# Wider pieces for the first two tiles of an input projection, norm weights by DMA, low parts on VectorE, and other PSUM places where the search begins

## The chip, the cores and the metric

The kernel runs on one core of a Trainium2 chip. Its engines are TensorE (PE; its weight loads are listed as PEld), VectorE (DVE), ScalarE (ACT), GpSimd (POOL) and SyncE (SP, which issues most transfers). The metric is the device time of one execution in microseconds; the time of a kernel is the median of its runs.

## The reference

One layer of a streaming-encoder block on 4096 tokens of width 1024, in float32:

```python
h = rms_norm(x, norm_g[layer])
proj = h @ w_in[layer]
q, k, v, qi, ki, wi, z_a, u_b, z_b, gates = jnp.split(proj, SPLIT_POINTS, axis=-1)
q = apply_partial_rope(rms_norm(q, q_norm_g[layer]), cos_a, sin_a)
k = apply_partial_rope(rms_norm(k, k_norm_g[layer]), cos_a, sin_a)
qi = apply_partial_rope(qi, cos_i, sin_i) * (IDX_DIM ** -0.5)
ki = apply_partial_rope(ki, cos_i, sin_i)
a = dsa_attention(q, k, v, qi, ki, wi, k_sel) * jax.nn.silu(z_a)     # top 256 keys of each query
b = multiscale_pool(u_b, pool_w, pool_scale) * jax.nn.silu(z_b)
y = g[:, :, 0] * (a @ w_branch_a) + g[:, :, 1] * (b @ w_branch_b)    # g: sigmoid of the gates
x = x + y @ w_out
```

The change lies in the first two lines, and there in the columns of q (512), k and v (256) and of the indexer (qi, ki and wi, 296).

## The kernel before, in words

The program has four phases: phase 1 (norm, and the projections to q, kv and the indexer's columns), the search (phase_index: index scores, the threshold of the top 256, and beside it the projections to gates and pools), attention, and output. Phase 1 goes over 32 tiles of 128 tokens.

Each float32 product is made from parts: a high part, rounded to the type that TensorE reads (F32R), and the low part that is left. A tile's h is in `hh` (high) and `hl` (low), weights are in `wqh`, `wql`, `wkvh`, `wkvl`, `wih`, `wil`; a product is hh·wh + hl·wh + hh·wl. With 1024 rows, eight k-steps of 128, each of the three is a pass of eight matmuls.

A tile t goes like this. `load_x` fetches x. `stats` squares it on ScalarE (`sq`, L451), takes the root (`rsqrt`, L383 to L390) and scales x on VectorE by that and by the norm weights `gn` (L460). `transp` turns it in two halves on TensorE (L473, into PSUM tiles `pt`), copies each half to `hh` on ScalarE (L475) and the rest to `hl` on VectorE (L476); SP stores both to `hD`. Then come the matmuls into the PSUM tiles `ma` (q and kv, 768 of 1024 columns) and `mb` (indexer), and `evac` reads these out: squares for the head norms (L548), the root (on POOL), the scaling L557, which is the last reader of `ma`, the rotation on POOL (L573 to L576) with the tables `trig`, and stores. `ma`, `mb` and `pt` have two places each, so tile t + 2 needs what tile t has left.

Tiles 2 to 31 multiply whole parts (`project`, `mm3`: 512, 256 and 296 columns in a matmul, L401 to L403). For tiles 0 and 1 the weights are still arriving: `weights` loads them in pieces of 128 columns (L502; the last one has 40), splits each into high (ScalarE, L503) and low (L506; for q's pieces 0 and 2 on POOL, for the others on VectorE), and `piece` multiplies piece by piece (L524).

`begin` does what comes ahead: constants, 18 matmuls of zeros (L301), and the norm weights, which are loaded as one row (L306, ScalarE's queue), spread over the partitions by two TensorE matmuls with a row of ones (L311, into a tile of `ma`) and copied to `gn` (L313). `tables` makes the cos and sin tables `trig` by a chain of VectorE instructions (L341 to L373) and a sine on ScalarE (L376).

The order of the instructions on each engine is set by `Plan`: each step has an engine, a cost in estimated microseconds and a key; a list scheduler goes through time, and whenever an engine is free it takes the step with the lowest key whose inputs and tiles are there. Engines then run their rows strictly in that order. PSUM places of phase 1 are given out as tiles are first made: before, `pt0` has bank 0, `ma0` banks 1 and 2, `pt1` bank 3, `ma1` 4 and 5, `mb0` and `mb1` 6 and 7. The search lays its own PSUM tiles over these in the order of the loop over `pl.have` in `phase_index`; a step on such a tile waits for the last reader of what lay there. `pd` holds the gate projections (L1196 to L1198), `ps` the scores.

## Time and profile before

| | us |
|---|---|
| runs (3) | 4132.86, 4133.96, 4137.76; median 4133.96 |
| profiled execution, its time | 4135.42 |
| its span, first to last instruction | 4133.7 |
| mean granted TensorE clock | 0.985 |
| tile 2 of phase 1 begins on TensorE | 73.91 |
| phase 1's last matmul | 452.47 |
| the search's first gate matmul | 456.48 |

Instruction rows give start, length, engine, line, operation, tiles out<-in, shapes and, in brackets, the idle time ahead and what ended it. A row's length on TensorE overlaps the next row's; the rate is read from the starts. Tables by stage give the busy time of each engine in a window, with the granted TensorE clock as a share of full speed.

### The profile page before, as it was taken

What the parts mean: (1) busy time and instruction counts of PE and PEld (TensorE: products, weight loads), DVE (VectorE), ACT (ScalarE), POOL (GpSimd) and SP (SyncE); (2) the same over time, 40 slices, a digit from 0 to 9 for tenths busy, and PEclk for the clock granted to TensorE, in tenths of its full rate; (3) what the DMA queues carried; (4) which work ended last, traced back from release to release, by engine and by line L of the source; (5) the groups of instructions that cost most, each with busy time, mean ns of one, the idle gap of its engine ahead of it and who ended that gap; (6) DMA issues with size and microseconds to landing.
All of it is one profiled execution on the core that took longest, in us unless ns stands there. A gap on an engine that the chain in (4) does not pass through costs nothing.

```text
span 4133.7 us, 64472 instructions
## 1 busy us (share of the span) xinstructions
PE 4012.3 (97%) x23202; PEld 3074.1 (74%) x23203; DVE 3251.7 (79%) x6399; ACT 2259.5 (55%) x3163; POOL 2022.9 (49%) x1618
## 2 busy tenths in 40 slices
PE   9999999999999999999989999999999999999999
PEld 9999888787777777788756666666666666887787
DVE  5555688888888888778779999999999996556654
ACT  4444578786777877877645555555554543111221
POOL 3555312212213223010018889999999994334653
PEclk9999999999999999999979999999999999999999
DMA  6876644544545345666554433333222215887543
GB/s 183 301 244 237 201 168 173 171 167 168 177 164 194 135 172 180 199 234 237 199 142 87 76 76 61 64 62 54 56 54 43 40 25 167 284 254 239 190 158 122
DMA packets 515846, 636.87 MB, mean 154 GB/s; under 512 B 230593, under 2 KB 365377, under 8 KB 511554
## 3 DMA queue, kind: packets, MB, share of 16 engines
q1 hardware_dynamic: 490432, 609.51, 47.1%
q10 hardware_dynamic: 25090, 23.21, 2.5%
q8 instruction: 183, 3.00, 0.3%
q14 instruction: 141, 1.16, 0.1%
HBM read 408.96 MB, written 191.76 MB: 145 GB/s over the span
## 4 chain that ended last, share of the span: by engine, by line
PE 37%; DVE 6%; issue 4%; DMA 1%; POOL 1%; SPq 1%; ACT 0%; ACTq 0%; DVEq 0%; POOLq 0%
PE pv L1686 9%; PE st L1634 8%; PE p L2139 7%; PE p L1990 7%; PE ps L1566 4%; DVE jk L1575 4%; DVE tt L1647 1%; PE pt L1734 1%; PE pt L395 1%; DMA qm<-maxD 1%; PE st L395 0%; PE st L1854 0%; POOL g L2020 0%; DVE w L1897 0%; DMA g<-w_out 0%
## 5 line engine op out<-in xcount | busy, mean ns | idle before, releaser
L1665 POOL TENSOR_TENSOR acc<-acc,tt 128x1024 f32<-128x1024 f32 x388 | 927.7, 2391 | 64.0 <-ACT tt L1646 36.9
L1646 ACT ACTIVATE tt<-tt 128x1024 f32<-128x1024 f32 (+1 forms) x544 | 561.1, 1034 | 549.7 <-DVE tt L1647 518.9
L1197 PE MATMUL pd<-h,wgh 128*128 128x512 f32 x1792 | 708.8, 396 | 9.9 <-DMA h<-hD 9.9
L1196 PE MATMUL pd<-h,wgh 128*128 128x512 f32 x1792 | 714.1, 399 | 3.9 <-issue 3.8
L908 DVE SCALAR_TENSOR_TENSOR ring<-rl,wi,ring 128x1024 f32<-128x1024 f32 (+7 forms) x624 | 702.1, 1170 | 15.7 <-ACT rl L906 12.4
L1198 PE MATMUL pd<-h,wgl 128*128 128x512 f32 x1792 | 707.0, 395 | 0.0
L906 ACT ACTIVATE rl<-ps 128x1024 f32<-128x1024 f32 (+7 forms) x624 | 535.5, 887 | 190.0 <-PE ps L903 69.4
L1647 DVE TENSOR_TENSOR tt<-st,bT 128x1024 f32<-128x1024 f32 (+1 forms) x504 | 600.8, 1193 | 13.1 <-PE st L1634 13.1
L993 ACT ACTIVATE sg<-ring,tk 128x2048 fp8e4<-128x2048 f32 (+9 forms) x322 | 485.1, 1508 | 63.0 <-DVE tk L981 34.4
L1686 PE MATMUL pv<-tt,vv 128*64 128x256 f32 x4224 | 516.2, 386 | 1.4 <-ACT ov L1707 1.4
L1575 DVE CUSTOM_DVE_ANT_1 jk<-ps,bias,mf 128x1024 bf16<-128x1024 f32 (+3 forms) x408 | 469.6, 1151 | 17.1 <-PE ps L1566 15.3
L1686 PEld LDWEIGHTS pv<-tt,vv 128*64 128x64 f32 x4224 | 286.5, 137 | 168.7 <-issue 35.4
L1197 PEld LDWEIGHTS pd<-h,wgh 128*128 128x128 f32 x1792 | 339.8, 190 | 84.1 <-DMA h<-hD 16.6
L1196 PEld LDWEIGHTS pd<-h,wgh 128*128 128x128 f32 x1792 | 340.0, 190 | 78.6 <-issue 4.2
L1198 PEld LDWEIGHTS pd<-h,wgl 128*128 128x128 f32 x1792 | 339.4, 189 | 75.9
L903 PE MATMUL ps<-kis,qT 128*128 128x512 f32 (+3 forms) x1136 | 345.3, 390 | 37.9 <-ACT rl L906 37.7
L1990 PE MATMUL p<-g,w 128*128 128x512 f32 x1488 | 345.5, 394 | 1.7 <-DVE g L1913 1.7
L1990 PEld LDWEIGHTS p<-g,w 128*128 128x128 f32 x1488 | 279.4, 188 | 67.6 <-DVE g L1913 2.1
L2139 PE MATMUL p<-w,g 128*128 128x512 f32 x1344 | 314.3, 396 | 4.0 <-ACT g L2143 3.1
L2139 PEld LDWEIGHTS p<-w,g 128*128 128x128 f32 x1344 | 253.5, 189 | 64.6 <-ACT g L2143 3.5
L1566 PE MATMUL ps<-kh,qh 64*128 64x512 f32 (+3 forms) x1320 | 265.5, 419 | 29.3 <-DVE mf L1575 26.5
L1110 POOL COPY halo<-u 128x16 f32<-128x16 f32 x32 | 11.2, 350 | 575.5 <-ACT u L1104 575.5
(364 smaller groups left out, 7012.3 us busy)
## 6 DMA issues: line engine op xcount, KB each, us to landing
h<-hD SPq DMA_DIRECT2D x384, 512.0 KB
g<-gD SPq DMA_DIRECT2D x80, 512.0 KB
hlD<-rhl SPq DMA_DIRECT2D x31, 1216.0 KB
gD<-sgm SPq DMA_DIRECT2D x128, 256.0 KB
q<-hlD SPq DMA_DIRECT2D x61, 512.0 KB
x<-x SPq DMA_DIRECT2D x32, 512.0 KB
hD<-hh SPq DMA_DIRECT2D x32, 512.0 KB
hD<-hl SPq DMA_DIRECT2D x32, 512.0 KB
```

Of the source, the lines that this page charges most:

```text
L906: r = pl.add("act", 0.05 + n * 0.834e-3, k_, lambda ps=ps, rl=rl, n=n: act.activation(rl.t[:, :n], ps.t[:, :n], AF.Relu), [m], use=[ps, rl])
L908: prev[o] = pl.add("dve", 0.1 + n * 1.04e-3, k_, lambda rl=rl, o=o, n=n, h=h: v.scalar_tensor_tensor(acc[:, o:o + n], rl.t[:, :n], self.wi ...
L1196: pe.matmul(out, wh.t[:, k], r1, start=(k == 0), stop=False)
L1197: pe.matmul(out, wh.t[:, k], r2, start=False, stop=False)
L1198: pe.matmul(out, wl.t[:, k], r1, start=False, stop=(k == KT - 1))
L1575: v.tensor_tensor_reduce(out=jk.t[:, :2 * (hi - lo) * P].rearrange("p (t n) -> p t n", t=2), in0=flat().rearrange("p (t n) -> p t n", t=2) ...
L1646: act.activation(tt.t[:, 0:n], tt.t[:, 0:n], AF.Exp)
L1647: ad = last_ve[0] = pl.add("dve", 0.07 + 0.54 * n, key, lambda: v.tensor_tensor(tt.t[:, 0:n], s.t[:, 0:n], bc(bt.t[:, 2 * p:2 * p + n, Non ...
L1665: gp.tensor_tensor(acc.t, first, tt.t, op=OP.add)
L1686: pe.matmul(pv.t[64 * f:64 * f + 64], vv[:, k, 64 * g:64 * g + 64], T[u, p].t[:, k % 2, 2 * f:2 * f + 2], start=(k == 0), stop=(k == b))
L1990: pe.matmul(p.t, blk[i].t[:, k, ms], two(x[k // 2][j].t, F32R)[:, k % 2], start=(k == i == j == 0), stop=(k == 3 and i == 1))
L2139: pe.matmul(p.t, quarter(Q.t, x, F32R)[:, k], blk[y].t[:, k], start=(fresh and k == x == y == 0), stop=(k == 3 and x == 1), skip_group_che ...
```

## The change

Pieces are still loaded and split by 128 columns, but for tiles 0 and 1 `piece` now takes a list of them: q in two halves of 256, kv whole (256), the indexer's columns whole (296). A pass over high weights waits for the highs of its pieces, the low pass for their lows. All lows are on VectorE. The norm weights come by one DMA on SP's queue that reads the row 128 times into `gn`; the row of ones, the two matmuls and the copy are gone. The loads of x1 to x3 stand at other places among the weights. The search's PSUM tiles are laid out in another order.

```diff
-ON_POOL = {("q", 0), ("q", 2)}
...
-        row = xp.tile([1, P], F32, name="onerow")
-        s = pl.add("dve", 0.2, -100, lambda: (v.memset(one, 1.0), v.memset(row, 1.0)))
+        s = pl.add("dve", 0.1, -100, lambda: v.memset(one, 1.0))
...
-        x, ma = new("x"), new("ma")
-        g = pl.add("dma", 0.1, -101, lambda: act.dma_start(x.t[0:1], a["norm_g"]), use=[x])
-
-        def spread():
-            for f in range(2):
-                fs = slice(f * 512, f * 512 + 512)
-                pe.matmul(ma.t[:, fs], row, x.t[0:1, fs], start=True, stop=True)
-        g = pl.add("pe", 1.8, -60, spread, [g, s], use=[x, ma])
-        return pl.add("dve", 1.2, -60, lambda: v.tensor_copy(gn, ma.t), [g], use=[ma])
+        return pl.add("dma", 1.7, -95, lambda: dma(gn, bass.AP(tensor=a["norm_g"].tensor, offset=a["norm_g"].offset,
+                                                              ap=[[0, P], [1, D]])))
...
-                on = "pool" if (key, j) in ON_POOL else "dve"
-                eng = {"dve": v, "pool": po}[on]
-                l = pl.add(on, (2.4 if on == "pool" else 1.15) * n + 0.1, at, lambda: eng.tensor_tensor(
+                l = pl.add("dve", 1.15 * n + 0.1, at, lambda: v.tensor_tensor(
                     lo[:, :, o:e], raw, hi[:, :, o:e].bitcast(F32), op=OP.subtract), [h])
...
-            def piece(t, key, j, at, prev):
+            def piece(t, key, js, at, prev):
                 m, c = out_of(t, key)
-                o, e, hi, lo = pieces[key][j]
+                parts = [pieces[key][j] for j in js]
+                o, e = parts[0][0], parts[-1][1]
+                hi, lo = [x[2] for x in parts], [x[3] for x in parts]
...
-                for i, (x, w, after) in enumerate(((hh, wh, high + [hi]), (hl, wh, low), (hh, wl, [lo]))):
+                for i, (x, w, after) in enumerate(((hh, wh, high + hi), (hl, wh, low), (hh, wl, lo))):
...
-                    prev = pl.add("pe", 8 * 0.5e-3 * max(e - o, 64), at, mm, after + [prev], use=[m, hh, hl])
+                    prev = pl.add("pe", 8 * 0.4575e-3 * (e - o), at, mm, after + [prev], use=[m, hh, hl])
...
-            first = (("q", 0), ("q", 1), ("x", 1), ("q", 2), ("q", 3), ("x", 2), ("kv", 0), ("kv", 1), ("x", 3), ("i", 0), ("i", 1),
-                     ("i", 2))
+            first = (("q", 0), ("q", 1), ("q", 2), ("x", 1), ("q", 3), ("kv", 0), ("kv", 1), ("x", 2), ("i", 0), ("i", 1),
+                     ("i", 2), ("x", 3))
...
-            for n, (key, j) in enumerate(x for x in first if x[0] != "x"):
+            for n, (key, js) in enumerate((("q", (0, 1)), ("q", (2, 3)), ("kv", (0, 1)), ("i", (0, 1, 2)))):
                 for t in range(2):
-                    last[t] = piece(t, key, j, n + t * 2.5, last[t])
-                    if (key, j) == ("kv", 1):
+                    last[t] = piece(t, key, js, 2 * n + t * 2.5, last[t])
+                    if key == "kv":
                         ends[t] = last[t]
-                if key == "kv":
-                    transp(2, j, n + 2.0)
-                elif key == "i" and j < 2:
-                    transp(3, j, n + 4.0)
+                        transp(2, t, 2 * n + t + 2.0)
+                    elif key == "i":
+                        transp(3, t, 2 * n + t + 4.0)
...
-        for name, i in (("ps", 0), ("pd", 0), ("pd", 1), ("pd", 2), ("pt", 0), ("ps", 1)):
+        for name, i in (("pt", 0), ("pd", 0), ("pd", 1), ("pd", 2), ("ps", 0), ("ps", 1)):
```

What the scheduler makes of it shows in the order of the rows. From tile 2's first matmul on, TensorE's rows are the same as before one for one; on the other engines the rows differ for a few tiles more and are then the same to the end. TensorE from the matmuls of zeros on, first before and then now (names carry the number of the place; `hh1` and `hl0` are tile 0's):

```order
L301 MATMUL pt0_146<-hh0_138 128x512 x4
L311 MATMUL ma0_154<-x0_140,onerow_103 128x512 x2
L301 MATMUL pt0_146<-hh0_138 128x512 x14
L473 MATMUL pt1_193<-ident_68,x1_142 128x128 x4
L473 MATMUL pt0_202<-ident_68,x1_142 128x128 x4
L524 MATMUL ma1_213<-wqh_104,hh1_194 128x128 x8
L524 MATMUL ma1_213<-wqh_104,hl0_195 128x128 x8
L524 MATMUL ma1_213<-wql_105,hh1_194 128x128 x8
```

```order
L299 MATMUL pt0_142<-hh0_136 128x512 x18
L464 MATMUL pt1_181<-ident_68,x0_138 128x128 x4
L464 MATMUL pt0_189<-ident_68,x0_138 128x128 x4
L515 MATMUL ma0_203<-wqh_103,hh1_182 128x256 x8
L515 MATMUL ma0_203<-wqh_103,hl0_183 128x256 x8
L515 MATMUL ma0_203<-wql_104,hh1_182 128x256 x8
```

The two matmuls on the row of ones are gone from among the zeros, the passes are twice as wide, and tile 0 is in `ma0` instead of `ma1`, so that tile 31 is in `ma1` instead of `ma0`. With no matmul into `ma0` ahead of the first transposes, `pt1` also gets bank 1, `ma0` banks 2 and 3.

TensorE where phase 1 ends and the search begins, before and now, with the engines and queues that a row waits for:

```order
L403 MATMUL mb1_5465<-wih_108,hl1_5144 128x296
L395 MATMUL mb1_5465<-identr_69,rhk2_5292 128x128 [waits DVE_49]
L1196 MATMUL pd0_5599<-h0_128,wgh0_5277 128x512 [waits DMAHW7_49,DVE_49,Activation_49]
L1197 MATMUL pd0_5599<-h1_129,wgh0_5277 128x512 [waits DMAHW1_49]
L1198 MATMUL pd0_5599<-h0_128,wgl0_5278 128x512
L395 MATMUL pt0_5603<-identr_69,k30_73 128x128
```

```order
L394 MATMUL mb1_5218<-wih_107,hl1_4897 128x296
L386 MATMUL mb1_5218<-identr_69,rhk2_5045 128x128 [waits DVE_49]
L1186 MATMUL pd0_5352<-h0_127,wgh0_5030 128x512 [waits DMAHW1_49]
L1187 MATMUL pd0_5352<-h1_128,wgh0_5030 128x512 [waits DMAHW2_49]
L1188 MATMUL pd0_5352<-h0_127,wgl0_5031 128x512
L386 MATMUL pt0_5356<-identr_69,k30_73 128x128 [waits DVE_49,PE_49]
```

The rows are the same; `pd0` lay on bank 2, the kv half of tile 31's `ma0`, and lies on bank 1, which was `pt1`. Its first matmul no longer waits for VectorE and ScalarE. `pd1` and `pd2` lie on banks 2 and 3 (now tile 30's `ma0`), the first `ps` on tile 31's `ma1`.

VectorE in the middle of the table chain (`ang`, `nh`, `nl`), before and now, with the low part of tile 3's h (`hl0`):

```order
L357 SCALAR_TENSOR_TENSOR ang_122<-nh_124,ang_122 128x384
L357 SCALAR_TENSOR_TENSOR ang_122<-nl_125,ang_122 128x384
L476 TENSOR_TENSOR hl0_792<-pt1_790,hh1_791 128x512
L360 SCALAR_TENSOR_TENSOR ang_122<-n_123,ang_122 128x384
L476 TENSOR_TENSOR hl0_792<-pt0_824,hh1_791 128x512
L363 COPY r2_126<-ang_122 128x32x12
```

```order
L323 TENSOR_SCALAR gqk_79<-gq_119 128x512
L324 COPY gqk_79<-gq_119 128x128
L348 SCALAR_TENSOR_TENSOR ang_121<-nh_123,ang_121 128x384
L348 SCALAR_TENSOR_TENSOR ang_121<-nl_124,ang_121 128x384
L467 TENSOR_TENSOR hl0_562<-pt1_560,hh1_561 128x512
L467 TENSOR_TENSOR hl0_562<-pt0_568,hh1_561 128x512
```

Tile 3's lows stood after six of the `ang` steps and now stand after two, so that four of them, and all that follows in the chain, come behind tile 3's transposes.

## The prediction

> **What bounds the kernel now.** I read the page's busy shares, then the stages, then TensorE's rows in order of time, since an engine with 97% over 4.1 ms says nothing on the first 75 us, where the change lies.

> ```profile
> PE 4012.3 (97%) x23202; PEld 3074.1 (74%) x23203; DVE 3251.7 (79%) x6399; ACT 2259.5 (55%) x3163; POOL 2022.9 (49%) x1618
> ```

> By stages (window in us, its length, busy time of each engine with instruction counts, granted TensorE clock, DMA share, GB/s):

> ```profile
> 5.00:20.00 15.00, 14.50 (x76) 10.82 (x74) 11.20 (x19) 8.06 (x14) 4.77 (x2) 1.00 1.13 320
> 14.00:53.50 39.50, 39.44 (x353) 39.26 (x352) 24.76 (x44) 15.77 (x29) 6.62 (x17) 1.00 0.63 183
> 53.50:55.40 1.90, 1.90 (x20) 1.90 (x18) 1.76 (x5) 0.87 (x2) 0.00 (x0) 0.99 0.61 209
> 55.40:75.80 20.40, 20.40 (x94) 20.01 (x94) 3.14 (x7) 3.07 (x6) 1.89 (x3) 0.50 0.05 5
> 75.80:440.00 364.20, 364.20 (x2332) 332.77 (x2331) 205.32 (x413) 173.52 (x431) 203.39 (x521) 1.00 0.75 259
> 452.70:456.40 3.70, 0.00 (x0) 0.00 (x0) 2.20 (x6) 1.75 (x9) 1.63 (x11) 0.77 0.48 195
> 456.50:461.50 5.00, 5.00 (x12) 3.86 (x13) 3.61 (x7) 1.98 (x6) 4.84 (x10) 0.50 0.16 57
> 500.00:720.00 220.00, 220.00 (x975) 179.41 (x974) 182.73 (x448) 175.32 (x199) 36.85 (x33) 1.00 0.46 166
> ```

> TensorE has work without a break from 14 us to 452.7, and again from 500 to 720. So what is saved ahead of tile 2 is kept, unless another engine falls behind. But from 55.4 to 75.8 the granted clock is 0.50, and a busy TensorE there is half a TensorE. What a matmul costs is read from start to start (the rows' own lengths overlap):

> ```profile
> 33.99 1.05 PE L524 MATMUL ma<-wqh,hh 128*128 128x128 f32 x8
> 41.14 1.06 PE L524 MATMUL ma<-wql,hh 128*128 128x128 f32 x8
> 42.03 0.62 PE L473 MATMUL pt<-ident,x 128*128 128x128 f32 x4
> 42.41 1.09 PE L524 MATMUL mb<-wih,hh 128*128 128x128 f32 x8
> 53.58 1.01 PE L524 MATMUL mb<-wih,hh 128*128 128x40 f32 x8
> 54.44 0.82 PE L524 MATMUL mb<-wih,hl 128*128 128x40 f32 x6
> 73.91 0.78 PE L401 MATMUL ma<-wqh,hh 128*128 128x512 f32 x1
> 87.45 0.39 PE L401 MATMUL ma<-wqh,hh 128*128 128x512 f32 x1
> 100.07 0.46 PE L401 MATMUL ma<-wqh,hh 128*128 128x512 f32 x1
> 440.76 0.44 PE L401 MATMUL ma<-wqh,hh 128*128 128x512 f32 x1
> 446.30 0.28 PE L401 MATMUL ma<-wkvh,hh 128*128 128x256 f32 x1
> 449.17 0.30 PE L401 MATMUL mb<-wih,hh 128*128 128x296 f32 x1
> 452.47 0.22 PE L395 MATMUL mb<-identr,rhk 128*128 128x128 f32 x1
> ```

> Eight passes of eight 128-column matmuls lie between 33.99 and 41.14: 0.894 us a pass, 112 ns a matmul. A pass of 40 columns costs as much (53.58 to 54.44: 0.86). Tile 31 has 24 matmuls of each width: 512 columns 231 ns (440.76 to 446.30), 256 columns 120 ns (to 449.17), 296 columns 137 ns (to 452.47). So a piece of 256 costs 8 ns more than one of 128. Four transposes cost 0.38 (42.03 to 42.41). Tiles 2, 3 and 4 begin at 73.91, 87.45 and 100.07: 12.62 a tile, and 0.9 more in tile 2, which begins at the low clock.

> [...]

> **The change, part by part.** *Wide pieces.* Before, two tiles took 48 passes of 128 columns and 6 of 40; now 18 of 256 (0.957) and 6 of 296 (1.10), 23.8 us. When can they run? The rows that time the start:

> ```profile
> 4.56 1.06 ACT L451 ACTIVATE sq<-x 128x1024 bf16<-128x1024 f32 x1 [1.51 <-DMA x<-x]
> 7.16 1.23 DVE L313 COPY gn<-ma 128x1024 f32<-128x1024 f32 x1 [5.34 <-PE ma L311]
> 9.68 3.62 DVE L460 SCALAR_TENSOR_TENSOR x<-x,rs,gn 128x512 f32<-128x512 f32 x2
> 9.71 2.39 POOL L506 TENSOR_TENSOR wql<-h,wqh 128x1024 fp32r<-128x1024 f32 x1 [8.15 <-ACT wqh L503]
> 15.65 1.05 ACT L503 ACTIVATE wqh<-h 128x1024 fp32r<-128x1024 f32 x1
> 19.79 0.75 DVE L460 SCALAR_TENSOR_TENSOR x<-x,rs,gn 128x512 f32<-128x512 f32 x1
> 20.46 1.22 DVE L506 TENSOR_TENSOR wql<-h,wqh 128x1024 fp32r<-128x1024 f32 x1
> 21.32 0.60 ACT L475 ACTIVATE hh<-pt 128x512 fp32r<-128x512 f32 x1 [2.55 <-PE pt L473]
> 22.32 0.68 DVE L476 TENSOR_TENSOR hl<-pt,hh 128x512 fp32r<-128x512 f32 x1
> ```

> x0 lands at 4.56; at 320 GB/s each 512 KB behind it takes 1.64 us. In SP's new order that puts the norm weights at 6.2, q0 to q2 at 7.8, 9.5 and 11.1, x1 at 12.8, q3 at 14.4, kv at 16.0 and 17.7, x2 at 19.3, the index columns by 23.1, x3 at 24.8. ScalarE in its new order (1.05 a split, 0.60 a turned half): first splits done 8.9, turned tile 0 at 10.6, q1 11.7, q2 12.7, square of x1, q3 at 15.9, kv 17.1 and 18.8, turned tile 1 by 19.4. VectorE: from the copy's end at 8.39 to the scaling at 9.68 the root chain takes 1.3; without that copy x0 is scaled by 8.5; the lows of q1 and q2 are done by 14.4, x1 is scaled by 18.4. TensorE: three passes 11.7 to 14.6, a wait for q3 to 15.9, q's other three and tile 1's transposes (the last at 18.8) to 19.75. From there nothing it needs is late: 12 passes of 256, 6 of 296, 4 times 0.38 make 19.6, so tile 2 begins at 39.4 instead of 73.91, at full clock, and tile 3 at 52.0 instead of 87.45: **35.4 us earlier**. Bounds: 36 if only q3's split held it (15.9 plus 23.2 of work left); 31.5 if every landing is 1.64 late and a half-clock stretch like that of 456.5 to 461.5 costs 2.2 (6.1 less 3.9, below).

> *Norm weights by DMA.* 512 KB ahead of the weights instead of 4 KB, two TensorE matmuls and a copy. Nearest row: an x tile, 1.64 us, already in the landings (between 0, if 128 reads of one row are cheap, and 3.3). *Lows on VectorE.* Two of 2.39 on POOL become two of 1.22 on VectorE (counted above); POOL no longer slows VectorE, whose two scalings took 3.62 beside POOL's first low instead of 2 x 0.75. *SP* moves x1 to x3 behind weights and the first hD stores; their landings are counted.

> *What is late next.* The cos/sin tables (VectorE) and tile 2's read-out, which frees the PSUM tile that tile 4 needs:

> ```profile
> 49.70 0.17 DVE L341 CAST pos<-pos_i 128x32 f32<-128x32 int32 x1
> 55.98 0.56 DVE L357 SCALAR_TENSOR_TENSOR ang<-nl,ang 128x384 f32<-128x384 f32 x1
> 75.53 0.35 DVE L363 COPY r<-ang 128x384 f32<-128x384 f32 x1
> 81.61 0.55 DVE L373 TENSOR_SCALAR r<-r 128x768 f32<-128x768 f32 x1
> 83.24 0.85 ACT L376 ACTIVATE trig<-r 128x768 f32<-128x768 f32 x1
> 93.69 0.81 DVE L557 TENSOR_TENSOR row<-ma,ss 128x640 f32<-128x640 f32 x1
> ```

> Now the table is there at 84.1 and tile 2's PSUM free at 94.5, 10.4 later, with tile 4 at 100.07: 5.6 of slack. After: the tables begin behind hl of tile 2's second half (transposed at 34.9, so 36.7), take 6.8 (49.70 to 56.54), 0.6 and 6.6 (75.53 to 82.16), less the 1.0 of sums of squares that now stands earlier, plus two hl of 0.68: 51.1; ScalarE's table load and sine end at 53.1; PSUM is free at 63.5, and tile 4 wants it at 39.4 + 25.2 = 64.6. That leaves 1.1, and POOL beside VectorE can take it: **1 us lost** (0 to 4). Behind TensorE's wait there, all of phase 1 is queued.

> *PSUM at the search's begin.*

> ```profile
> 455.55 0.82 DVE L557 TENSOR_TENSOR row<-ma,ss 128x640 f32<-128x640 f32 x1 [1.18 <-POOL ss L390]
> 456.48 0.76 PE L1196 MATMUL pd<-h,wgh 128*128 128x512 f32 x1 [3.78 <-issue]
> 461.77 0.40 PE L1196 MATMUL pd<-h,wgh 128*128 128x512 f32 x1
> ```

> pd0 lay on tile 31's ma0, so its first matmul began 0.1 after L557 had read it (456.37), and the idle 3.8 cost the clock as well. Now pd0 lies on pt1, free long before. From 452.6, 12 matmuls at 231 ns and a transpose bring TensorE at 455.7 to where it was at 461.77: **6.1 us** (3.9 if the clock falls anyway; 0 if a later step waits for tile 31's chain). I take 6.1: pd1 and pd2 lie on tile 30's tile, and from 500 to 720 TensorE is busy 220.00 of 220.00.

> Sum: -35.4 + 1 - 6.1 = -40.5. The profiled execution took 4135.42 (span 4133.7, 1.7 around it), 1.5 over the median; 4094.9 against it, **4094** against the median. For: every term comes from rows at the same clock.

> **Rivals.**
> 1. *The table chain binds*, through POOL holding up VectorE (9.68 beside 9.71): tile 4 waits some 5 us, with a half-clock window behind it. Against: the slack worked out is positive. 4101.
> 2. *The clock falls all the same.* At 53.5 it falls while TensorE is busy 1.90 of 1.90; if running long, not narrow matmuls, does that, 20.4 us at half clock come again, and 10.2 of gain is lost: 4104. Against: it held from 14 to 53.5 with 128 columns, fell in the first 40-column passes, and came back within 2 us of the 512-column ones at 73.91. [...]
> 3. *The search begins no earlier than before*, since its own chain from tile 31 (sums, table loads) ends last: the 6.1 go: 4100. Against: 500 to 720.
> 4. *Slower: transfers set phase 1's pace.* Before, the queue rested from 55.4 to 75.8 (share 0.05); now no rest precedes tile 2, and the share is 0.75 at 12.62 us a tile. It turns slower if each of 30 tiles waits over 1.35 us for x; at 1.7 it ends at 4094 + 51 = 4145. Against: 364.20 busy of 364.20 with a quarter of the transfers' time free.
> 5. *No change*: whole pieces of 256 wait for two loads and two lows each, and the first two tiles end where they did, at 73.9: 4133. Against: the last index load lands by 23.1.

> **Numbers.** Forecast 0.60 (its own range 4090 to 4098: the start's bounds but for late loads, the stall's 0 to 4), rival 1 0.15, 2 0.12, 3 0.08, 4 0.03, 5 0.02. 4087 to 4107 takes in the forecast and rivals 1 to 3, and leaves out some 0.12 with their tails. 0.2% (8 us) is about what a measurement of this kernel can tell from no change; all of the forecast and rivals 1 to 3 lie beyond it: faster 0.95, same 0.02, slower 0.03.

> **What would show it.** Tile 2's first matmul at 38 to 42 us and tile 3's 12.6 later; granted clock 1.00 from 14 to 440; tile 4's begin 25.2 after tile 2's (more is rival 1); no TensorE gap over 0.5 us where phase 1 ends, and clock 1.00 there. A tile 2 later than 45, a clock of 0.50 for 20 us, or gaps of over a microsecond at many tiles would make it wrong.

## The result and the profile after

The changed kernel takes **4091.23 us** (median of 4 runs, 4087.19 to 4092.13) against 4133.41 before (4 runs, 4128.5 to 4137.76): a ratio of **0.9896, 95% interval 0.9879 to 0.9914**, 42.2 us less. The profiled execution took 4092.13, its span is 4090.4. The forecast was 4094, its range 4087 to 4107.

The page's first part, after:

```profile
PE 3967.6 (97%) x22958; PEld 3030.5 (74%) x22959; DVE 3249.0 (79%) x6399; ACT 2257.2 (55%) x3163; POOL 2021.6 (49%) x1616
```

TensorE is busy 44.7 us less, with 244 fewer matmuls in the record; the sums of VectorE, ScalarE and GpSimd stay within 3 us. By stages after (window, length, busy time of PE, PEld, DVE, ACT, POOL with counts, granted clock, DMA share, GB/s):

```profile
11.70:15.10 3.40, 3.40 (x19) 3.40 (x18) 2.80 (x7) 2.68 (x5) 0.00 (x0) 0.50 1.17 302
15.20:38.90 23.70, 23.54 (x196) 23.33 (x195) 18.88 (x33) 15.01 (x29) 5.19 (x18) 1.00 0.98 300
64.00:66.00 2.00, 0.78 (x5) 0.35 (x3) 2.00 (x6) 1.88 (x7) 1.75 (x8) 1.00 0.94 371
66.00:418.00 352.00, 352.00 (x2246) 320.51 (x2247) 197.37 (x388) 160.59 (x411) 196.60 (x501) 1.00 0.75 261
418.00:428.00 10.00, 10.00 (x49) 8.08 (x47) 6.85 (x14) 4.79 (x17) 6.85 (x20) 1.00 0.26 100
```

The 20.40 us at half clock are gone (one window of 3.4 us is at 0.50 instead, at 11.7), and so is the idle time where phase 1 ends. New is the hole at 64 to 66. TensorE's rows after: first pass, fourth pass, two low and high passes, tile 2, tile 3, the hole ahead of tile 4, the search's begin, the first scores.

```profile
11.00 1.52 PE L515 MATMUL ma<-wqh,hh 128*128 128x256 f32 x8 [1.65 <-ACT wqh L494]
15.79 1.20 PE L515 MATMUL ma<-wqh,hh 128*128 128x256 f32 x8 [0.16 <-ACT wqh L494]
24.16 1.07 PE L515 MATMUL ma<-wkvl,hh 128*128 128x256 f32 x8
25.07 1.10 PE L515 MATMUL ma<-wqh,hh 128*128 128x256 f32 x8
38.90 0.48 PE L392 MATMUL ma<-wqh,hh 128*128 128x512 f32 x1
51.58 0.39 PE L392 MATMUL ma<-wqh,hh 128*128 128x512 f32 x1
64.72 0.28 PE L386 MATMUL pt<-identr,rhk 128*128 128x128 f32 x1 [0.41 <-DVE hl L467]
66.00 0.50 PE L392 MATMUL ma<-wqh,hh 128*128 128x512 f32 x1 [0.81 <-DVE row L548]
418.70 0.22 PE L386 MATMUL mb<-identr,rhk 128*128 128x128 f32 x1
418.76 0.44 PE L1186 MATMUL pd<-h,wgh 128*128 128x512 f32 x1
435.00 0.63 PE L893 MATMUL ps<-kis,qT 128*128 128x512 f32 x2
```

The first scores stood at 474.64 before:

```profile
474.64 0.63 PE L903 MATMUL ps<-kis,qT 128*128 128x512 f32 x2
```

So where the 43.3 us between the two profiled spans come from can be followed row by row: 35.0 are there at tile 2 (73.91 to 38.90), 35.9 at tile 3, 34.1 at tile 4 (the hole costs 1.8), 33.8 at tile 31 (440.76 to 406.98), 39.6 at the first scores (474.64 to 435.00; so 5.9 from the boundary). The last 3.6 arise in the 3.65 ms behind, whose instructions did not change.

Eleven of the kernels, each from the trace of one run (us; "rest" is from the first scores to the end, "half" the time at clock 0.50 in it by the clock record):

| kernel | median | tile 2 | tile 4 after tile 2 | first scores | rest | half |
|---|---|---|---|---|---|---|
| before | 4133.4 | 73.91 | 26.16 | 474.64 | 3659.0 | 95.6 |
| after | 4091.2 | 38.90 | 27.10 | 435.00 | 3655.4 | 81.9 |
| wide_only | 4103.7 | 43.52 | 25.41 | 442.54 | 3659.1 | 99.5 |
| order_only | 4131.7 | 73.28 | 26.78 | 474.85 | 3660.0 | 99.0 |
| norm_by_matmul | 4107.4 | 46.88 | 25.28 | 445.89 | 3664.7 | 102.4 |
| lows_on_gpsimd | 4094.4 | 39.23 | 26.50 | 434.52 | 3657.6 | 97.4 |
| old_order | 4093.9 | 38.93 | 26.48 | 436.52 | 3654.6 | 83.0 |
| early_tables | 4096.1 | 39.35 | 29.64 | 440.02 | 3658.6 | 93.3 |
| tables_after_x3 | 4088.1 | 39.94 | 25.35 | 434.73 | 3650.6 | 71.7 |
| n40 | 4128.0 | 67.92 | 26.38 | 463.06 | 3656.0 | 82.5 |
| n128 | 4112.0 | 60.97 | 25.30 | 455.45 | 3653.5 | 81.9 |

The column "rest" varies by 14 us over kernels that are alike there, and goes with "half": over these 11 and three more profiles the correlation is 0.91, the slope 0.34 us for each us at half clock. So the 3.6 us behind the first scores are most simply scatter of the clock (13.7 us less at half clock in that one execution), no effect of the change (argued, not tested); what the change did is read at the first scores, where single profiles tell differences that the medians cannot.

### The profile page after: what moved, and what is told of

The parts are those of the page before. It is cut to its first block, busy times and chain, and to the rows that moved or that the text cites. A ratio compares the mean times of both kernels' runs of the same rounds, so it can differ in the third digit from the quotient of the medians.

```text
span 4090.4 us, 63978 instructions
## 1 busy us (share of the span) xinstructions
PE 3967.6 (97%) x22958; PEld 3030.5 (74%) x22959; DVE 3249.0 (79%) x6399; ACT 2257.2 (55%) x3163; POOL 2021.6 (49%) x1616
## 4 chain that ended last, share of the span: by engine, by line
PE 67%; DVE 15%; issue 7%; ACT 4%; DMA 4%; POOL 1%; SPq 1%; ACTq 0%; DVEq 0%; POOLq 0%
PE pv L1676 9%; PE st L1624 8%; PE p L2129 7%; PE p L1980 7%; PE pd L1187 6%; PE pd L1186 6%; PE pd L1188 6%; DVE jk L1565 4%; PE ps L893 4%; PE ps L1556 4%; DVE ring L898 3%; ACT sg L983 2%; PE ma L392 2%; PE ma L393 2%; PE ma L394 2%
## 5 line engine op out<-in xcount | busy, mean ns | idle before, releaser
L1637 DVE TENSOR_TENSOR tt<-st,bT 128x1024 f32<-128x1024 f32 (+1 forms) x504 | 600.8, 1193 | 13.8 <-PE st L1624 13.7
L1556 PE MATMUL ps<-kh,qh 64*128 64x512 f32 (+3 forms) x1320 | 265.1, 419 | 29.3 <-DVE mf L1565 26.5
L893 PEld LDWEIGHTS ps<-kis,qT 128*128 128x128 f32 x1136 | 206.1, 188 | 117.2 <-ACT rl L896 77.4
```

What stands on the lines that cost most here:

```text
L893: pe.matmul(ps.t[:, s:e], t.t[:, h], self.kis[:, o + s:o + e], start=True, stop=True)
L1637: ad = last_ve[0] = pl.add("dve", 0.07 + 0.54 * n, key, lambda: v.tensor_tensor(tt.t[:, 0:n], s.t[:, 0:n], bc(bt.t[:, 2 * p:2 * p + n, Non ...
```

## Experiments

### Is it the width, and what lost the clock? (n40, n128)

n40 is the changed kernel with the old loop over pieces:

```diff
-            for n, (key, js) in enumerate((("q", (0, 1)), ("q", (2, 3)), ("kv", (0, 1)), ("i", (0, 1, 2)))):
+            for n, (key, j) in enumerate(x for x in first if x[0] != "x"):
                 for t in range(2):
-                    last[t] = piece(t, key, js, 2 * n + t * 2.5, last[t])
+                    last[t] = piece(t, key, (j,), n + t * 2.5, last[t])
...
```

> The changed kernel, but the first two tiles multiply in pieces of 128 columns again (the indexer's last one 40); loads, norm weights, low parts and PSUM places as changed. Theory (narrow matmuls cost a whole weight load each, and the passes of 40 columns lose the clock): from a first pass at 10.0 us, 48 passes of 0.894, 6 of 0.86 and 6 times four transposes of 0.38 would end at 60.4; the first 40-column passes come at about 49, the granted clock falls to 0.50 within 4 us of them and stays there to tile 2's 512-column matmuls, so tile 2 begins at 68 to 70 and the time is about 4121. Rival 1 (only the number of passes counts, the fall before had another cause): clock 1.00, tile 2 at 60 to 62, 4113. Rival 2 (something else held the start, such as the loads' order): tile 2 as now at 39, 4091. No TensorE gap over 0.5 us where phase 1 ends in any case.

n128 differs from it only in the columns of the last piece:

```diff
+                if (key, js) == ("i", (2,)):
+                    js = (1, 2)
                 parts = [pieces[key][j] for j in js]
                 o, e = parts[0][0], parts[-1][1]
+                if key == "i" and len(js) == 2:
+                    o = e - 128
```

> As the kernel with narrow pieces, same passes in the same order, but the indexer's last piece is 128 columns wide instead of 40: it computes 88 columns a second time into the same place. Theory (the 40-column passes lose the clock): granted clock 1.00 up to tile 2, which begins at 60 to 62; time about 4113. Rival 1 (a long run of narrow passes loses it, whatever their width): the clock falls at 50 to 55 us as before, tile 2 at 68 to 70, 4121. Rival 2 (a fixed window of the clock at about 55 us whatever runs): a fall at 55 here and none in the changed kernel only by chance; 4116 to 4121.

TensorE in n40, the passes of 40 columns and those behind them, and by stages:

```profile
49.43 1.02 PE L515 MATMUL mb<-wih,hh 128*128 128x40 f32 x8
51.18 1.05 PE L515 MATMUL mb<-wil,hh 128*128 128x40 f32 x8
52.08 1.09 PE L515 MATMUL mb<-wih,hh 128*128 128x128 f32 x8
54.48 1.91 PE L515 MATMUL mb<-wil,hh 128*128 128x128 f32 x8
56.19 1.91 PE L515 MATMUL mb<-wih,hh 128*128 128x128 f32 x8
67.92 0.78 PE L392 MATMUL ma<-wqh,hh 128*128 128x512 f32 x1
```

```profile
49.40:53.20 3.80, 3.80 (x36) 3.80 (x36) 2.60 (x7) 1.64 (x4) 0.22 (x1) 1.00 0.48 164
53.30:67.90 14.60, 14.60 (x71) 14.60 (x71) 2.09 (x6) 1.70 (x5) 0.06 (x1) 0.50 0.00 1
```

And n128, where the same passes stand in the same order:

```profile
49.40:61.00 11.60, 11.60 (x107) 11.60 (x106) 8.07 (x16) 4.27 (x10) 1.99 (x2) 1.00 0.15 53
```

```profile
60.97 0.48 PE L392 MATMUL ma<-wqh,hh 128*128 128x512 f32 x1
```

The theory holds on both counts. With 40 columns the clock falls at 53.24, 3.8 us behind the first such pass, with TensorE busy 3.80 of 3.80; a pass then takes 1.71 instead of 0.89, and tile 2 comes at 67.92, just ahead of the 68 to 70 expected. With 128 columns in these passes there is no fall, and tile 2 comes at 60.97. So of the 29 us between n40 and the changed kernel 7 are the clock, 22 the narrow passes themselves. That the weight load sets the pace of a narrow matmul is the author's estimate: loads were busy 3.80 of 3.80 us in 49.40:53.20, but also 23.33 of 23.70 beside the 256 columns of the changed kernel. The medians were 4128.03 and 4112.03, ratios to before 1.0001 (0.9973 to 1.0029) and 0.9985 (0.9946 to 1.0023): wider than the profiles, since the runs of each fall in two groups (n40: seven at 4120.5 to 4128.4, three at 4157 to 4164; n128: seven at 4104 to 4120, three at 4157 to 4163). The next runs point to a cause for that.

### How narrow is too narrow? (n64, n96, n64_again)

The same edit with `o = e - 64` and `o = e - 96`.

> As the kernel with narrow pieces, but the indexer's last piece is 64 columns wide (24 computed a second time). By 0.434 ns a column (512 against 256 columns: 231 and 120 ns) the array streams for 15% of a 112 ns matmul with 40 columns and for 50% with 128; with 64 it is 25%. Theory (the clock is kept by the share of a window in which the array streams, with a bound somewhere between 15 and 50%): below the bound the clock falls to 0.50 at 50 to 55 us and tile 2 begins at 68; above it, clock 1.00 and tile 2 at 61. I expect the fall. Rival (only passes of very few columns count): no fall, 61.

> The same with 96 columns in the last piece, 37% of a matmul's time. Theory: a fall and tile 2 at 68 if the bound lies above 37%, else 1.00 and tile 2 at 61; I expect it held. Rival as for 64 columns: 61.

In n64's profile (4161.95) the clock was lost long before the 64-column passes, so that it says nothing on them, but something else. By stages:

```profile
9.40:12.80 3.40, 2.93 (x23) 2.72 (x23) 3.38 (x5) 2.68 (x4) 0.00 (x0) 1.00 1.13 335
12.90:61.00 48.10, 48.10 (x229) 48.10 (x229) 13.61 (x24) 11.20 (x19) 2.54 (x8) 0.50 0.50 145
61.00:104.70 43.70, 43.70 (x208) 43.70 (x207) 9.68 (x20) 5.86 (x14) 2.75 (x10) 0.50 0.13 37
```

In 9.40 to 12.80 TensorE was idle 0.47 us, at the first waits for hh and hl. The clock fell at 12.85, and 92 us of dense matmuls (128 columns, behind 61 us some of 64, and transposes) did not bring it back; tile 2 came at 104.73, and its 512-column matmuls brought it back at 108.4. The waits alone do not explain the fall: in the same stretch n128 and n96, shown in this order, were idle 0.43 and 0.46 us at the same rows and kept the clock:

```profile
9.40:12.80 3.40, 2.97 (x23) 2.76 (x24) 3.39 (x5) 2.64 (x4) 0.00 (x0) 1.00 1.13 335
9.40:12.80 3.40, 2.94 (x23) 2.73 (x23) 3.37 (x5) 2.67 (x4) 0.00 (x0) 1.00 1.13 335
```

What decided is not shown. So passes of 128 columns kept a clock that was there (n128: 1.00 from 12.00 to 61.00) and did not win it back (n64: 0.50 over the 48.10 us from 12.90); in the changed kernel, where it is lost at 11.69 as well, the 256-column passes have it back by 15.11. The run with 96 columns held it (4111.19, one run):

```profile
12.00:61.00 49.00, 49.00 (x443) 49.00 (x443) 25.56 (x48) 18.37 (x35) 6.78 (x18) 1.00 0.61 181
```

Its first three 96-column passes ran from 49.49 to 52.15. Whether 96 columns hold the clock in every run is not shown by this one.

> The kernel with 64 columns in the last piece once more, since in its first run the clock had been lost at 12.85 us already, before any 64-column pass, and stayed at 0.50 for 95.57 us (4162). Theory 1 (128-column passes hold the clock where they have it, and do not win it back): some runs lose it at the start and take 4157 to 4163, as 3 in 10 runs of each of the kernels with 40 and with 128 columns did; in the others the start is at 1.00. In those, if 64 columns (25% of a matmul's time) keep it, tile 2 begins at 61 and the runs take 4104 to 4120 as with 128 columns; if they lose it, tile 2 begins at 68 and the runs take 4120 to 4128 as with 40. Rival (that first run was a disturbed one): no run over 4140.

This time the start kept its clock and the 64-column passes (49.39 to 52.04) lost it, as 40 columns did:

```profile
49.30:53.20 3.90, 3.90 (x38) 3.90 (x36) 2.64 (x7) 1.83 (x4) 0.21 (x1) 1.00 0.52 183
53.30:67.80 14.50, 14.50 (x71) 14.50 (x71) 2.08 (x5) 1.50 (x5) 0.01 (x1) 0.50 0.00 1
```

Ten runs: seven at 4118 to 4129, three at 4158 to 4162; median 4123.59, ratio 1.0008 (0.9977 to 1.0039). Three in ten once more, at the time that n64's profiled run took: that these upper groups are all runs which lost the clock at the start is likely from their distance (n64's tile 2 comes 37 to 44 us later than that of the others), and shown for one run only.

### What is the PSUM order worth? (old_order, order_only)

```diff
-        for name, i in (("pt", 0), ("pd", 0), ("pd", 1), ("pd", 2), ("ps", 0), ("ps", 1)):
+        for name, i in (("ps", 0), ("pd", 0), ("pd", 1), ("pd", 2), ("pt", 0), ("ps", 1)):
```

> The changed kernel with the search's PSUM tiles laid out in the old order; rows of every engine unchanged. pd0 then lies on bank 2, the q half of tile 30's tile, and pt0 on bank 5, the kv half of tile 31's. Theory (what counts is which place of tile 31's tile the first steps of the search lie on): three gate matmuls run at once (0.7 us), then the turn into pt0 waits for tile 31's scaling on VectorE, a gap of about 3 us, perhaps with a half-clock window of 2 us behind it; the search's scores come 3 to 5 us later than in the changed kernel; 4094 to 4096. Rival (the shift of tile 31 to the other place alone did it, the order is worth nothing): no gap over 0.5 us at 427 us, 4091.

In order_only the same line is edited the other way, in the kernel before.

> The kernel before with only the new order of the search's PSUM tiles. pd0 then lies on bank 1, the q half of tile 31's tile, which is in ma0 here. Theory (the gap goes only if tile 31 lies in the other place as well, which it does once the norm weights no longer take a place of ma): the gap of 3.8 us at 452.7 and the half-clock stretch stay, 4133. Rival (the order alone does it): no gap over 0.5 us, clock 1.00 there, the scores 6 us earlier, 4127.

TensorE where phase 1 ends, in old_order and in order_only:

```profile
421.41 0.25 PE L386 MATMUL pt<-identr,k 128*128 128x128 f32 x1 [2.38 <-DVE row L548]
```

```profile
456.27 0.77 PE L1196 MATMUL pd<-h,wgh 128*128 128x512 f32 x1 [3.58 <-issue]
456.83 0.63 PE L1197 MATMUL pd<-h,wgh 128*128 128x512 f32 x1
```

Both theories hold in kind. The new order alone is worth nothing (ratio 0.9998, 0.9988 to 1.0008; the gap of 3.58 and the half clock behind it stay). With the old order in the changed kernel the gap moves from `pd` to `pt` and is 2.38 us, without a fall of the clock. From tile 31's begin to the first scores it is 33.9 us before, 34.1 in order_only, 30.2 in old_order and 28.0 in the changed kernel: 3.7 come with tile 31's other place, 2.2 more with the order on top of it (3 to 5 were expected from old_order). The median of old_order, 4093.86 (0.9899, 0.9878 to 0.992), cannot tell this from the changed kernel.

### Which of the start's edits count? (wide_only, norm_by_matmul, lows_on_gpsimd)

wide_only is the kernel before with the new `piece` and its loop alone.

> The kernel before with only the wide pieces: norm weights by matmul, q's lows 0 and 2 on GpSimd, loads and PSUM places as before. Theory (width brings nearly all of the start's gain): first pass at about 14 as before, then 18 passes of 256, 6 of 296 and the turned halves, 26 us without a break, so tile 2 begins at 40 to 42; granted clock 1.00 from 14 to phase 1's end; the gap of 3.8 us and the half-clock stretch at phase 1's end stay; some 2 us lost at tile 4; time 4101 to 4104. Rival (norm weights by DMA and lows on VectorE bring part of it): tile 2 after 45 us, 4106 or more.

It took 4103.74 (0.9939, 0.9918 to 0.996), with tile 2 at 43.52, a little late, and the gap in its place, but with no half-clock stretch behind it:

```profile
426.77 0.47 PE L1197 MATMUL pd<-h,wgh 128*128 128x512 f32 x1 [3.36 <-issue]
```

So width alone brings 30.4 of the 35.0 us at tile 2; the other start edits bring 4.6. Whether a gap of 3.4 to 3.8 us costs the clock is not sure either: it did in before (3.78), order_only (3.58) and norm_by_matmul (3.69), not here (3.36; 2.8 us less from tile 31 to the scores than before).

norm_by_matmul is the changed kernel with the row of ones, the two matmuls and the copy again:

```diff
-        return pl.add("dma", 1.7, -95, lambda: dma(gn, bass.AP(tensor=a["norm_g"].tensor, offset=a["norm_g"].offset,
-                                                              ap=[[0, P], [1, D]])))
+        x, ma = new("x"), new("ma")
+        g = pl.add("dma", 0.1, -101, lambda: act.dma_start(x.t[0:1], a["norm_g"]), use=[x])
...
+        g = pl.add("pe", 1.8, -60, spread, [g, s], use=[x, ma])
+        return pl.add("dve", 1.2, -60, lambda: v.tensor_copy(gn, ma.t), [g], use=[ma])
```

> The changed kernel with the norm weights by one row, two matmuls and a copy again; all else as changed. The matmuls take a place of ma, so tile 31 lies in ma0 again, under pd0. Theory: 512 KB less ahead of the weights, but x0 is scaled 2.5 us later behind the copy, so tile 2 begins at 38.5 to 41, near the changed kernel's 38.9; at phase 1's end the gap of 3.8 us and a half-clock stretch of 5 to 7 us come back, and the scores start 6 us later: about 4097. Rival (the norm weights' edit counts at the start, not at the end): tile 2 about 1.6 us earlier, no gap at the end, 4089.

4107.42 (0.9942, 0.9923 to 0.9962). The end came out as expected (a gap of 3.69 and a half-clock stretch), the start not: tile 2 at 46.88, 8 us later than with the DMA. VectorE shows why:

```profile
9.68 0.75 DVE L459 SCALAR_TENSOR_TENSOR x<-x,rs,gn 128x512 f32<-128x512 f32 x1
10.35 2.35 DVE L503 TENSOR_TENSOR wql<-h,wqh 128x1024 fp32r<-128x1024 f32 x2
14.00 0.69 DVE L475 TENSOR_TENSOR hl<-pt,hh 128x512 fp32r<-128x512 f32 x1 [1.29 <-ACT hh L474]
14.94 1.23 DVE L503 TENSOR_TENSOR wql<-h,wqh 128x1024 fp32r<-128x1024 f32 x1 [0.25 <-ACT wqh L502]
16.09 0.75 DVE L459 SCALAR_TENSOR_TENSOR x<-x,rs,gn 128x512 f32<-128x512 f32 x1
```

The second half of x0 is scaled 6.4 us behind the first: with all lows on VectorE the scheduler had put two of them, a low part of h and a third low between. TensorE's second turn waits for it:

```profile
16.98 1.09 PE L472 MATMUL pt<-ident,x 128*128 128x128 f32 x4 [3.65 <-DVE x L459]
```

The clock fell with that wait, to 0.50 from 15.61 to 22.43, so the first three passes ran at half speed as well. This run prices the norm weights' edit together with a row order that it makes; the copy alone was to cost 2.5.

lows_on_gpsimd has q's lows 0 and 2 on GpSimd again (`ON_POOL = {("q", 0), ("q", 2)}`), all else as changed.

> The changed kernel with the lows of q's pieces 0 and 2 on GpSimd again. Theory (beside a GpSimd low VectorE's steps wait: two scalings took 3.62 us there before, 1.41 now): if the low runs beside x0's scalings, x0 is ready 2.2 us later and tile 2 begins at 40.5 to 41.5; if it runs beside x1's, about 1 us; time 4092 to 4094. Rival (VectorE, freed of 2.4 us, makes up for it): tile 2 at 38.5 to 39, 4091. At phase 1's end as in the changed kernel.

Tile 2 at 39.23, first scores at 434.52, 4094.38 (0.9913, 0.9896 to 0.9929): nothing that can be told. The theory's condition did not come about, so that it is not tested: VectorE and GpSimd rows,

```profile
7.06 1.42 DVE L452 SCALAR_TENSOR_TENSOR x<-x,rs,gn 128x512 f32<-128x512 f32 x2
...
9.12 2.36 POOL L498 TENSOR_TENSOR wql<-h,wqh 128x1024 fp32r<-128x1024 f32 x1 [7.56 <-ACT wqh L495]
```

x0 is scaled by 8.48, before GpSimd begins at 9.12; they no longer meet.

### Can the hole ahead of tile 4 be closed? (early_tables, tables_after_x3)

```diff
-        c = pl.add("dma", 0.5, key - 14, lambda: dma(self.cst, a["cst"]))
+        c = pl.add("dma", 0.5, -83.5, lambda: dma(self.cst, a["cst"]))
...
-        ld = pl.add("dma", 0.3, key - 13, load)
+        ld = pl.add("dma", 0.3, -83.4, load)
```

> The changed kernel with the loads of the cos and sin tables' inputs (cst, positions, head norm weights) issued ahead of x2 instead of after x5, so that the chain of table steps on VectorE begins at about 21 us instead of 37.5. Theory (tile 4 waits because the tables' chain holds up tile 2's read-out): the sine ends 8 to 10 us earlier than at 56.15, tile 4 begins 25.2 to 25.4 us after tile 2 instead of 27.1, no TensorE gap over 0.2 us there; 1.8 us less, about 4089. Rival (another wait takes its place: the last weights or x3 0.9 us later, or the rotations on GpSimd): tile 4 begins 26 us or more after tile 2, or tile 2 itself after 39.5; 4091 or above. The 2 us are less than the runs' spread, so the profile decides.

The sine came 3.7 us earlier, not 8 to 10, and tile 4 came later, 29.64 behind tile 2. VectorE and TensorE there:

```profile
63.31 2.54 DVE L451 SCALAR_TENSOR_TENSOR x<-x,rs,gn 128x1024 f32<-128x1024 f32 x1
65.78 2.29 DVE L598 TENSOR_TENSOR rhl<-row,rhl 128x512 fp32r<-128x512 f32 x3
67.99 0.68 DVE L467 TENSOR_TENSOR hl<-pt,hh 128x512 fp32r<-128x512 f32 x1
...
68.81 0.25 PE L386 MATMUL pt<-identr,rhk 128*128 128x128 f32 x1 [4.02 <-DVE hl L467]
```

The rival won: tile 2's read-out was done at 62.05, in time, but VectorE's new row has the next scaling and three splits ahead of the low half that frees a turned place, and TensorE waits 4.02 us for that; the clock fell with it, to 0.50 from 69.77 on for 3.41 us. The median was 4096.06 (0.9901, 0.9879 to 0.9922).

tables_after_x3 has -78.9 and -78.8 instead, right behind x3, by which the low half comes first.

> The changed kernel with the loads of the tables' inputs issued right behind x3. In the run with these loads ahead of x2 tile 4 came 29.6 us after tile 2 (27.1 in the changed kernel), because VectorE's new row put two long steps ahead of the low half that frees a turned place; here the row has that half first. Theory (tables late, and then the row's order): the sine ends about 4 us earlier than at 56.15, tile 2's read-out ends by 62, tile 4 begins 25.2 to 25.6 us after tile 2, 1.8 us less than the changed kernel, 4089. Rival (VectorE beside GpSimd has no room for it): tile 4 begins over 26.5 us after tile 2, 4091 or above.

Tile 4 came 25.35 behind tile 2, so the hole is closed. But tile 2 itself came at 39.94, 1.0 later, with short waits for VectorE in front of it (0.24 for hl, 0.35 for tile 0's read-out). First scores at 434.73 against 435.00: the wait moved, most simply because VectorE has no room there. The median of 4088.08 (0.990, 0.988 to 0.992) is not to be told from the changed kernel's 0.9896, and its profile has the shortest "rest" of all. No version that clearly beats the changed kernel came out of this.

## Why the prediction was right, step by step

- *Wide pieces, -35.4.* Measured -35.0 at tile 2 and -35.9 at tile 3, where the old low clock's 0.9 is in. Tile 2 was put at 39.4 and came at 38.90. The first pass began 0.7 earlier than worked out (11.00), a pass of 256 takes 0.91 to 0.93 instead of 0.957. The last thing that held TensorE was q3's split, as the chain of landings had it (15.9; the row has 15.79). The half-clock stretch at 11.7, which stood in the bounds only, cost nothing: in tables_after_x3 the start kept its clock, and the fourth pass began at 15.76 all the same.
- *Rival 2, the clock.* The reasoning that narrow matmuls, not a long run, had lost it was argued from one stretch; n40 and n64_again (0.50 behind passes of 40 and 64 columns, with TensorE busy 3.80 of 3.80 and 3.90 of 3.90) and n128 (1.00 with 128 columns in the same passes) show it.
- *Stall at tile 4, +1 (0 to 4).* Measured +1.8, at the place named; of the 1.22 us that TensorE is idle there, 0.81 are the wait named (tile 2's read-out) and 0.41 a wait for a low half of h. What was under-sized is VectorE's delay beside GpSimd:

```profile
41.37 1.80 DVE L348 SCALAR_TENSOR_TENSOR ang<-nl,ang 128x384 f32<-128x384 f32 x1
51.48 2.21 DVE L359 TENSOR_TENSOR r<-r,wrap 128x768 f32<-128x768 f32 x1
40.95 1.81 POOL L554 TENSOR_TENSOR row<-row,gqk 128x640 f32<-128x640 f32 x1 [1.89 <-DVE gqk L324]
51.06 1.81 POOL L554 TENSOR_TENSOR row<-row,gqk 128x640 f32<-128x640 f32 x1 [0.94 <-DVE row L548]
55.30 0.85 ACT L367 ACTIVATE trig<-r 128x768 f32<-128x768 f32 x1
65.14 0.81 DVE L548 TENSOR_TENSOR row<-ma,ss 128x640 f32<-128x640 f32 x1
```

  Two steps that take 0.55 and 0.96 elsewhere in the same chain stood beside GpSimd's multiplications of 1.81 (L554); that is 2.5 us, and the sine ended at 56.15 instead of 53.1, the read-out at 65.95 instead of 63.5. Each of the two ends 0.4 and 0.8 us behind GpSimd's, as if it had begun only when that was done; this is read from their times, and no run takes GpSimd's step away.
- *PSUM places, -6.1.* Measured -5.9. The price was right, the account of it short, and part of it was luck. The 6.1 holds some 2.2 for the clock that fell behind the gap, as if the gap must cost it; wide_only kept its clock over a gap of 3.36 and lost 2.8 us less. And the gain was given to pd0's place under the new order, but order_only shows that the order does nothing while tile 31 lies in the other place, and that comes from the norm weights' edit at the far end of the phase.
- *Norm weights and lows.* They had no term of their own beyond the landing; that x0 is scaled by 8.5 without the copy stood inside the chain of the start, whose whole gain went under the name of wide pieces. wide_only shows their share together with the loads' order: 4.6 us at tile 2, where the first pass begins at 14.04 instead of 11.00. How the 4.6 divide is not shown: norm_by_matmul made another row order, lows_on_gpsimd came within 0.3 of the changed kernel, and the loads' order was not changed alone. As the sum was made from the changed kernel's own chain, this did not hurt it.
- *The sum, -40.5.* -39.6 at the first scores. The rest of the 43.3 between the profiles lies in the scatter behind.
- *Rival 1* came in part, as the +1.8 above, with TensorE idle 1.22 us and no fall of the clock. *Rivals 3 to 5* did not come: no gap at the boundary, and TensorE is busy 352.00 of 352.00 from tile 4 to phase 1's end with a DMA share of 0.75.

## What to carry to other kernels

Where weights arrive in pieces, load them in pieces but multiply in wide ones (here a matmul took 110 ns with 40 columns, 112 with 128, 120 with 256 and 231 with 512). Judge a start by two things, the last landing that it needs and whether its matmuls are wide enough to win a lost clock back (here 256 columns did within 3.41 us, 128 did not in 48.10); and when an edit takes or gives back a place of a ring, look at the far end of the phase, where another tile will lie under the next phase's first step.
